# Moving tiles to one place of 512 bytes, and reordering the first loads and the last pair, in a hybrid GLA/HGRN2 encoder step

## The chip, the cores and the metric

The kernel runs on one core of a Trainium2 chip. The metric is the device time in microseconds of one execution; lower is better. Of the core's engines, TensorE (PE in the profile) multiplies matrices: one operand is loaded as weights (PEld), the other streams through in columns, and the result is added up in PSUM. VectorE (DVE), ScalarE (ACT) and GpSimd (POOL) do the elementwise work. Loads and stores between HBM and the on-chip memory SBUF are DMAs, issued from a queue of SyncE (SP) or of ScalarE. SBUF has 128 partitions; where a tile lies is one byte offset that holds in all partitions.

## The reference

One layer of an encoder with two parallel groups of heads runs over a prompt of 4096 frames and a sample of 64 frames, in float32. Cut to what matters:

```python
def mixer_layer(x, c, s_gla, s_hgrn, w_ada, b_ada, g_pre, w_in, w_alpha, b_alpha,
                g_on_gla, lb, g_on_hgrn, w_out, g_post):
    mod = jnp.einsum('bd,de->be', c, w_ada) + b_ada
    shift, scale, gate = jnp.split(mod, 3, axis=-1)
    h = rms_norm(x, g_pre) * (1 + scale[:, None]) + shift[:, None]
    p = jnp.einsum('btd,de->bte', h, w_in)          # 1024 -> 3600 columns
    q_a, k_a, v_a, z_a, a_lr, q_h, f_h, i_h, z_h = jnp.split(...)
    log_alpha = log_sigmoid(a_lr @ w_alpha + b_alpha) / GATE_TAU
    o_a, s_a = chunked_gla(q_a * GLA_DK ** -0.5, k_a, v_a, log_alpha, s_gla)
    f = lb + (1.0 - lb) * sigmoid(f_h)
    o_h, s_h = chunked_gla(silu(q_h), 1.0 - f, i_h, log(f), s_hgrn)
    o_a = rms_norm(o_a, g_on_gla) * silu(z_a)
    o_h = rms_norm(o_h, g_on_hgrn) * silu(z_h)
    o = jnp.einsum('bte,ed->btd', jnp.concatenate([o_a, o_h], axis=-1), w_out)
    return x + gate[:, None] * rms_norm(o, g_post), s_a, s_h
```

`chunked_gla` is a linear recurrence over frames, S = diag(exp g) S + k v, o = q S. The outputs are y for prompt and sample and the four final states.

## The kernel before

The prompt is cut into 16 groups of 256 frames, each of two tiles of 128; the sample's 64 frames go along with one group. There are four stages. The first group's projections run in `first_group`, written out by hand while the weights still arrive. Then 16 GLA groups, 16 HGRN2 groups, the gate z of the HGRN2 half for all tiles (`z_tile`), and the output projection (`project`), which works on pairs of frame tiles p = 0 to 15. A function `weave` mixes the projections of one group with the recurrence of the group before, so that TensorE always has matmuls at hand; within what is issued, a scheduler may still move instructions of different engines against each other.

Every product of h with a weight is made in three matmuls. `split` cuts a float32 operand into a rounded part and the rest (hi and lo, in float32r), and hi x hi, hi x lo and lo x hi are added up in PSUM. So every matmul loads 128 columns of weights anew. Two lines make most of the projections:

- L594 in `proj_feat`: loads 128 columns of the projection's weights (tiles `wa`, `wv`) and streams 256 frames of h (`hh`). GLA's q and k and HGRN2's f use `wa`, HGRN2's q uses `wv`.
- L606 in `tok_step`: loads 128 frames of h and streams the projection's weights, 512 columns (`wb`: v; `wa`: z of the last stage) or 264 (`wv`: z and the low-rank gate of GLA).

The output projection multiplies with seven products of 2x2 blocks instead of eight (a Strassen-Winograd scheme). `load_wout` makes the seven combinations of blocks of w_out (B11 to T4), each in four units of [128, 2 x 512], kept in freed `wv` and `wb` buffers and in twelve `wc`. `project` makes the combinations of the input (A11, A12, A22, S1 to S4) for each pair, in `wa` buffers (`s_tile`) and in two stage buffers `hs` (`a_tile`). L1391 in `product` is their matmul: it loads u, streams W. Each product fills one PSUM bank (`pj`, three deep, or `o`) in 12 matmuls. The last pair also holds the sample (`sample`, L614). `store` computes the norm over a row from the squares' sums, and adds x: sums (L1463), `rstd` (L82 to L93), L1472, and a DMA.

SBUF is handed out from two sides. From the left come `const`, `small`, the weights (`wa`, `wv`, `wb`, eight each), then the recurrence's tiles (later `wc` and the rest). From the right come the stage buffers, `e`, h (`hf`, `hh`) and x. A `wv` tile is 1056 words of 4 bytes, all other weights' tiles 1024; a stage buffer is 1056 words too. This puts the tiles, in bytes past a multiple of 512, at:

| tile | before |
|---|---|
| `hh`, `hf`, `xt`, `e` | 224 |
| `hs`, the two | 224, 352 |
| `wa`, `wb`, `wc`, recurrence (`A`, `K`, `v`, ...) | 320 |
| `wv`, eight buffers | 320, 448, 64, 192, twice over |
| `ident` (for transposes) | 128 |

hi and lo of one tile lie a multiple of 512 apart, but for the 264 columns, where the four pieces lie at 0, 32, 64 and 96 past the tile's place.

At the start, `setup` issues all loads on SP's queue: x, twelve small row vectors into `rows`, the identity, w_ada, and the first weights; small loads stand between the w_ada loads. `first_group` warms TensorE with matmuls on zeros (`warm`, L294), transposes the first 16 rows (L298), turns the first x tile (L313), then transposes all 52 rows (L319) into `col`, turns the second x tile, and goes on with the sums of w_ada (L241) and eight steps over k (L352, L606).

Of the kernel before, what the change touches and what calls it, by code (L numbers as in the profile page):

```python
# [6 lines left out]
F32 = mybir.dt.float32  # L7
F32R = mybir.dt.float32r
# [3 lines left out]
ALU = mybir.AluOpType  # L12
# [16 lines left out]
class Kernel:  # L29
# [41 lines left out]

    def rstd(self, ms, n, table=False):


        nc = self.nc
        r, w = ms.shape[0], ms.shape[1]
        yt = self.small.tile([P, 8], F32, name="nwt_y")
        ut = self.small.tile([P, 8], F32, name="nwt_u")
        mt = self.small.tile([P, 8], F32, name="nwt_m")
        y, u, m = yt[:r, :w], ut[:r, :w], mt[:r, :w]  # L80
        yi = yt.bitcast(I32)[:r, :w]
        nc.vector.tensor_scalar(m, ms, 1.0 / n, EPS, ALU.mult, ALU.add)  # L82
# [63 lines left out]
    def setup(self):  # L146
# [3 lines left out]
        self.wpool = self.pool(ctx, "w")  # L150

        self.wstage = self.pool(ctx, "wstage", 2, side="right")
        self.halves = []
# [14 lines left out]

        nc.scalar.preload_act_table_set("natural_log_exp_and_others")
        self.ident = c.tile([P, P], F32, name="ident")  # L170
# [16 lines left out]
        with ExitStack() as s:  # L187
            one = self.pool(s, "setup")
            ap = self.pool(s, "ada", 3)

            rows = one.tile([52, P], F32, name="rows")
            v = lambda a: a.rearrange("(k p) -> k p", p=P)
            self.x_load(0, [0])
            nc.sync.dma_start(rows[0:8], v(t["c_prompt"][0]))
            nc.sync.dma_start(rows[8:16], v(t["c_sample"][0]))
            nc.sync.dma_start(self.ident, t["ident"])
            self.x_load(0, [1])
            few = [
                (rows[16:32], v(t["b_ada"][0, : 2 * D])),
                (rows[32:40], v(t["g_pre"][0])),  # L200
                (rows[40:42], v(t["b_alpha"][0])),
                (rows[42:50], t["hgrn_lb_logits"].rearrange("r (k p) -> (r k) p", p=P)),
                (rows[50:51], t["g_onorm_gla"]),
                (rows[51:52], t["g_onorm_hgrn"]),
            ]
            ada = self.ada_load(ap, 0, few[:4])
            w = self.first_load(0)
            for dst, src in few[4:]:
                nc.sync.dma_start(dst, src)
            with self.tc.manual_schedule():  # L210
                self.first_group(ap, ada, w, rows)
            for _ in self.vs0:
                pass
# [3 lines left out]

    def ada_load(self, ap, k, few=()):

        sts = []  # L220
        for i in range(2):
            st = ap.tile([P, 4, 2, P], F32, name="ada_st", bufs=10)
            for e in range(2):
                src = self.t["w_ada"][0, i * 512 : i * 512 + 512, e * D + k * P : e * D + (k + 1) * P]
                self.nc.sync.dma_start(st[:, :, e, :], src.rearrange("(n p) c -> p n c", p=P))
                for dst, src in few[2 * i + e : 2 * i + e + 1]:
                    self.nc.sync.dma_start(dst, src)
            sts.append(st)
        return sts

    def first_group(self, ap, ada, w, rows):

# [59 lines left out]
        def warm(n):  # L292
# [4 lines left out]
        pr = self.ps("ms")  # L297
        nc.tensor.transpose(pr[:, :16], rows[:16], self.ident[:16, :16])  # L298
        warm(8)
        self.x_norm(0, [0])  # L300
        nc.vector.tensor_copy(col[:, :16], pr[:, :16])
        self.x_norm(0, [1])
        nc.vector.tensor_copy(
# [3 lines left out]
            self.fold4, self.ident.rearrange("p (n r) -> p r n", r=32)[:, 0:2], mybir.AxisListType.X, ALU.add  # L307
        )
        pts = [self.ps(n).rearrange("p (k t) -> p k t", k=2) for n in ("tp", "at", "at", "pj")]

# [6 lines left out]
        turn(0)  # L317
        pr = self.ps("ms")
        nc.tensor.transpose(pr[:, :52], rows, self.ident[:52, :52])  # L319
        turn(1)  # L320
# [3 lines left out]
        self.hf = [self.hp.tile([P, 2, T], F32, name="hf", bufs=4) for _ in range(4)]  # L324
        nc.vector.tensor_copy(col[:, 16:], pr[:, 16:52])
        nc.vector.tensor_scalar(col[:, 24:32], col[:, 24:32], 1.0, None, ALU.add)
        raw(0, nc.scalar)
        w_split(0, ws[0])
        am = ada_out(pa)
        ws.append(self.first_load(1))  # L330
# [11 lines left out]
        for k in range(KT):  # L342
# [31 lines left out]
            if k + 3 < KT:  # L374
                sts.append(self.ada_load(ap, k + 3))
            if k == KT - 3:
                self.x_load(1, [0, 1])
# [930 lines left out]
    def load_wout(self, room):  # L1308
# [62 lines left out]
    def project(self, ogs, rest):  # L1371

        nc, t, W = self.nc, self.t, self.W3
        ng = self.ng
        quarter = lambda u: u[:, :1024].rearrange("p (two k c) -> p two k c", two=2, k=4)
        s_tile = lambda: quarter(self.wunit("wa"))
        a_tile = lambda: quarter(self.stage_pair(F32R))

# [14 lines left out]
        with ExitStack() as s:  # L1393

            a21, a22 = [turn(o, n) for o, n in zip(ogs[2:], ("tp", "ms"))]
            a11, a12 = [turn(o, "at") for o in ogs[:2]]
            A11, A12 = a_tile(), a_tile()
            parts(A11, a11)
# [67 lines left out]
            def store(ss, ys, xs, dst, last=False):  # L1466

                r = ys[0].shape[0]
                add(ss[:r, 0:1], ss[:r, 0:1], ss[:r, 1:2])
                rs = self.rstd(ss[:r, 0:1], D, table=True)  # L1470
                for q in range(2):
                    nc.vector.scalar_tensor_tensor(xs[q], ys[q], rs, xs[q], ALU.mult, ALU.add)  # L1472
                    (nc.scalar if last and q else nc.sync).dma_start(dst[:, 512 * q : 512 * q + 512], xs[q])
# [26 lines left out]
            def sample(both, xs, gs):  # L1500
# [15 lines left out]
                store(ss, ys, xs, t["y_sample"][0, s0 : s0 + r])  # L1516

            ogs = og_load(1) if ng > 1 else None
            for p in range(ng):
# [8 lines left out]
                if more:  # L1528
# [4 lines left out]
                    add(w1, w21, a22)  # L1533

                b = self.ps("pj")
# [4 lines left out]
                if not more:  # L1540
                    sample(both, *rest_s)
                if more:
                    a11 = turn(ogs[0], "at")
                    A11 = a_tile()
                    w3, w2 = block(), block()
                    sub(w3, a11, w21)
                    sub(w2, w1, a11)
                    parts(A11, a11)
                    parts(S3, w3, nc.gpsimd)
                    parts(S1, w1, nc.gpsimd)  # L1550
                    parts(S2, w2)

                b = self.ps("pj")
                product(b, cur["S2"], "T2")
                u2 = add(tmp(), b, p1)
                if more:
                    A22, A12 = s_tile(), a_tile()
                    parts(A22, a22)
                    a12 = turn(ogs[1], "at")
                    parts(A12, a12)  # L1560
                    ogs = og_load(p + 2) if p + 2 < ng else None

                b = self.ps("pj")
                product(b, cur["S3"], "T3")
                u3 = add(tmp(), b, u2)
                if more:
                    S4 = s_tile()
                    w4 = sub(block(), a12, w2)
                    parts(S4, w4, nc.gpsimd)
                if p == ng - 2:  # L1570
# [19 lines left out]
                scale(y21, y21, 0)  # L1590
                store(ss[1], [y21, y22], xs[2:], rows(p, 1), not more)
                if p == ng - 2:
                    both = turn_sample(ogs)
                if more:
                    cur = dict(A11=A11, A12=A12, A22=A22, S1=S1, S2=S2, S3=S3, S4=S4)

# [207 lines left out]
```

## Time and profile before

| | us |
|---|---|
| time, median of 3 runs | 2065.14 (2062.38 to 2065.37) |
| time of the profiled execution | 2065.15 |
| its span | 2063.4 |
| granted TensorE clock, share of full speed | 0.995 |
| PE busy | 2033.4 (99%) |
| DVE busy | 1513.0 (73%) |
| ACT busy | 1088.9 (53%) |
| first matmul of the eight steps (L352) | at 19.0 |
| last matmul's end, by the chain | at 2054.4 |

The span runs from the first to the last instruction's record; the time has a little around it. Lines like L594 are those of the kernel before. A row such as `L594 PE MATMUL ps_pj<-hh,wa 128*128 128x256 f32 x2784 | 360.8, 284` reads: line, engine, operation, what it writes from what, the tile of weights, the shape streamed, how often; busy us in total, mean ns of one.  A row of the timeline has start, length, engine, line, operation, count, and in brackets how long the engine had been idle and what ended that. A row of the chain has start, length, and who led.

### The profile page before, as it was taken

To read this page: it belongs to the slowest core of one execution; us is meant where nothing else is said; L and a number is where in the kernel's file an instruction comes from. 1 tells how busy PE (TensorE), PEld (TensorE's weight loads), DVE (VectorE), ACT (ScalarE), POOL (GpSimd) and SP (SyncE) were. 2 spreads that over 40 slices of the span, in tenths; PEclk is the share of its full clock that TensorE was granted. 3 is DMA by queue.
4 is the path that set the end of the run, shared out by engine and by line. 5 is a ranking of instruction groups with operands and counts; after the bars stand their busy time and mean duration, and the time that the engine had idled before them with its cause. 6 is when DMAs were issued, how large, how long until landed. Compare 5 with 4: busy or idle time off the path is not lost.

```text
span 2063.4 us, 47068 instructions
## 1 busy us (share of the span) xinstructions
PE 2033.4 (99%) x17404; PEld 1796.0 (87%) x17404; DVE 1513.0 (73%) x4740; ACT 1088.9 (53%) x3207; POOL 304.1 (15%) x782
## 2 busy tenths in 40 slices
PE   8999999999999999999999999999999999999998
PEld 6888899999999888989999999999978888888886
DVE  4776777767777678777777877877786667767675
ACT  4676666777667565444444444444545544434332
POOL 0111111111111121111111111111110002333321
PEclk9999999999999999999999999999999999999999
DMA  9332222232222231011111111100246654534443
GB/s 296 97 77 64 62 58 57 64 73 62 58 56 75 82 118 44 32 37 60 52 37 51 46 65 32 38 32 32 63 139 212 216 194 149 170 131 167 140 143 103
DMA packets 236086, 190.10 MB, mean 92 GB/s; under 512 B 138208, under 2 KB 160196, under 8 KB 235856
## 3 DMA queue, kind: packets, MB, share of 16 engines
q1 hardware_dynamic: 235712, 186.83, 29.9%
q8 instruction: 137, 2.24, 0.5%
q14 instruction: 93, 0.76, 0.1%
q10 hardware_dynamic: 144, 0.26, 0.0%
HBM read 126.59 MB, written 60.43 MB: 91 GB/s over the span
## 4 chain that ended last, share of the span: by engine, by line
PE 91%; DVE 4%; ACT 3%; DMA 1%; issue 1%; POOL 0%; SPq 0%; DVEq 0%; ACTq 0%; POOLq 0%
PE ps_pj L606 32%; PE ps_pj L594 25%; PE ps_pj L1391 13%; PE ps_at L674 3%; PE ps_at L1003 2%; PE ps_ms L805 2%; PE ps_o L789 2%; PE ps_o L781 2%; PE ps_o L1391 2%; PE ps_at L910 1%; PE ps_tp L754 1%; PE ps_pj L614 1%; PE ps_at L1382 1%; PE ps_ms L781 1%; PE ps_pj L352 1%
## 5 line engine op out<-in xcount | busy, mean ns | idle before, releaser
L594 PE MATMUL ps_pj<-hh,wa 128*128 128x256 f32 (+1 forms) x2976 | 390.8, 286 | 0.6 <-ACT hh L102 0.4
L606 PE MATMUL ps_pj<-wb,hh 128*128 128x512 f32 x1536 | 386.0, 402 | 0.5 <-POOL wb L103 0.5
L594 PEld LDWEIGHTS ps_pj<-hh,wa 128*128 128x128 f32 x2976 | 369.1, 189 | 5.3 <-issue 1.7
L606 PEld LDWEIGHTS ps_pj<-wb,hh 128*128 128x128 f32 x1536 | 281.7, 189 | 66.1 <-issue 2.9
L594 PE MATMUL ps_pj<-hh,wv 128*128 128x256 f32 (+1 forms) x1536 | 196.2, 285 | 0.0
L594 PEld LDWEIGHTS ps_pj<-hh,wv 128*128 128x128 f32 x1536 | 187.4, 189 | 10.0 <-issue 9.7
L606 PE MATMUL ps_pj<-wv,hh 128*128 128x264 f32 x1464 | 191.1, 287 | 0.0
L606 PEld LDWEIGHTS ps_pj<-wv,hh 128*128 128x128 f32 x1464 | 181.5, 188 | 3.6 <-ACT e L1099 2.4
L606 PE MATMUL ps_pj<-wa,hh 128*128 128x512 f32 x768 | 182.3, 396 | 0.0
L606 PEld LDWEIGHTS ps_pj<-wa,hh 128*128 128x128 f32 x768 | 143.3, 188 | 35.0 <-issue 0.8
L1249 ACT ACTIVATE g<-ps_pj 128x256 f32<-128x256 f32 (+1 forms) x128 | 49.6, 388 | 219.3 <-PE ps_pj L594 214.3
L103 DVE TENSOR_TENSOR hh<-hf,hh 128x512 fp32r<-128x512 f32 (+1 forms) x188 | 129.9, 696 | 16.3 <-ACT hh L102 13.6
L102 ACT CAST hh<-hf 128x512 fp32r<-128x512 f32 (+1 forms) x188 | 117.2, 624 | 41.6 <-PE ps_pj L606 22.8
L816 DVE SCALAR_TENSOR_TENSOR S<-S,T,ps_ms 128x128 f32<-128x128 f32 x186 | 56.1, 340 | 81.4 <-PE ps_ms L805 81.4
L953 DVE TENSOR_TENSOR wst<-wst,T 128x160 f32<-128x160 f32 (+4 forms) x480 | 107.9, 265 | 1.4
L977 ACT ACTIVATE A<-Ac,member 128x128 f32<-128x128 f32 x256 | 80.0, 389 | 47.2 <-DVE Ac L971 47.2
L1451 ACT ACTIVATE sq<-e 128x512 bf16<-128x512 f32 x64 | 40.4, 631 | 121.0 <-DVE e L1463 121.0
L1391 PE MATMUL ps_pj<-wc,wa 128*128 128x512 f32 x384 | 98.9, 392 | 0.0
L1454 POOL TENSOR_TENSOR e<-e,gg 128x512 f32<-128x512 f32 x32 | 41.6, 1299 | 367.8 <-ACT sq L1451 367.8
L984 POOL COPY T<-T 128x16 f32<-128x16 f32 (+1 forms) x32 | 7.8, 244 | 543.7 <-DVE Qg L845 401.6
L1391 PEld LDWEIGHTS ps_pj<-wc,wa 128*128 128x128 f32 x384 | 72.0, 188 | 16.3
L971 DVE COPY_PREDICATED Ac<-mask,ps_at 128x112 f32<-128x112 uint8 (+6 forms) x448 | 82.5, 223 | 2.1 <-PE ps_at L1003 1.0
(349 smaller groups left out, 4028.2 us busy)
## 6 DMA issues: line engine op xcount, KB each, us to landing
hf<-h_d SPq DMA_DIRECT2D x128, 256.0 KB
h_d<-hf SPq DMA_DIRECT2D x64, 256.0 KB
oh_d<-e SPq DMA_DIRECT2D x64, 256.0 KB
xq<-in_x_prompt_dram SPq DMA_DIRECT2D x64, 256.0 KB
out_y_prompt_dram<-xq SPq DMA_DIRECT2D x63, 256.0 KB
xt<-in_x_prompt_dram SPq DMA_DIRECT2D x448, 32.0 KB
wst<-in_w_in_dram SPq DMA_DIRECT2D x36, 256.0 KB
e<-oh_d SPq DMA_DIRECT2D x33, 256.0 KB
```

The lines of the kernel that those rows point to most:

```text
L102: self.nc.scalar.copy(hi, src)
L103: (eng or self.nc.vector).tensor_tensor(lo, src, hi.bitcast(F32), ALU.subtract)
L594: self.nc.tensor.matmul(ps[:, :T], a, b, start=i == 0, stop=i == n - 1)
L606: self.nc.tensor.matmul(ps[:r, : c1 - c0], a, b, start=kt == 0 and i == 0, stop=kt == KT - 1 and i == 2)
L674: nc.tensor.transpose(pt[:, i * P : (i + 1) * P], D[:, c + i, :], self.ident)
L781: mm = nc.tensor.matmul(po[h], A[:, c * 4 + h, :], v, start=h < n, stop=St is None and h == 4 - n)
L816: nc.vector.scalar_tensor_tensor(Sn[:, g, :], St[:, g, :], T[:, c * G + g, 0:1], pd[:, g, :], ALU.mult, ALU.add)
L953: nc.vector.tensor_tensor(parts(dst), parts(src), t.unsqueeze(3).to_broadcast(shape), ALU.mult)
L971: nc.vector.copy_predicated(Ach[:, :, 4 * a :].rearrange("p h (j m) -> p h j m", m=4), self.mask[:CL, : 8 - a].unsqueeze(1).unsqueeze(3).t ...
L977: nc.scalar.activation(Ah[:, :, 32 * b : 32 * b + 32], Ach, AF.Copy, scale=self.member[:CL, 8 + b : 9 + b])
L1249: nc.scalar.activation(sg, pf[:, :T], AF.Sigmoid)
L1391: nc.tensor.matmul(bank, u[:, a, kt, :], W[name][kt][:, b], start=kt + i == 0, stop=kt + i == 5)
```

## The change

It has three parts.

*Places.* A tile `pad` of 32 bytes is put ahead of all others on the right side, so all tiles there move by -32. In `quad_norm`, `q_ss` and `q_half` have two buffers instead of four, four tiles of 32 bytes less in `small`, so all that lies behind on the left moves by -128. h, `wa`, `wb` and `wc` then lie at 192 past a multiple of 512, `wv` at 192, 320, 448, 64. In `load_wout` those parts of w_out that are kept in four of the eight `wv` buffers start 32 words (128 bytes) further in, and the second of `a_tile`'s two buffers too: by the order in which the buffers are taken, the units in `wv` lie at 192 or 448, and the two `hs` at 192 and 448.

*First loads.* c_prompt, c_sample, b_ada and g_pre go on ScalarE's queue, ahead of its table load. Their 40 rows stay in `rows` and are transposed once, ahead of the first x tile; the other 12 rows go to a tile `later`, loaded after the first weights and transposed in the second of the eight steps. Five warming matmuls stand between the two x tiles where the transpose stood. The copy of the sums (`ada_out`) is issued ahead of `w_split(0)`, and the second x tile's norm behind the work on `col`.

*Last pair.* A function `last` orders the products of pair 15 as A11 B11, S2 T2, (sample), S1 T1, S4 B22, A12 B21, S3 T3, A22 T4, instead of A11 B11, A12 B21, (sample), S2 T2, S3 T3, S1 T1, S4 B22, A22 T4. The first half of the rows is stored after A12 B21. For the last store, one half's sum of squares is scaled ahead, so that one VectorE operation adds the other (`rest` in `rstd`).

```diff
-    def rstd(self, ms, n, table=False):
+    def rstd(self, ms, n, table=False, rest=None):
...
-        nc.vector.tensor_scalar(m, ms, 1.0 / n, EPS, ALU.mult, ALU.add)
+        if rest is None:
+            nc.vector.tensor_scalar(m, ms, 1.0 / n, EPS, ALU.mult, ALU.add)
+        else:
+            nc.vector.scalar_tensor_tensor(m, ms, 1.0 / n, rest, ALU.mult, ALU.add)
...
+        self.pool(ctx, "pad", side="right").tile([P, 8], F32, name="pad")
         self.wstage = self.pool(ctx, "wstage", 2, side="right")
...
-        nc.scalar.preload_act_table_set("natural_log_exp_and_others")
...
-            rows = one.tile([52, P], F32, name="rows")
+            rows, later = one.tile([40, P], F32, name="rows"), one.tile([12, P], F32, name="later")
             self.x_load(0, [0])
-            nc.sync.dma_start(rows[0:8], v(t["c_prompt"][0]))
-            nc.sync.dma_start(rows[8:16], v(t["c_sample"][0]))
             nc.sync.dma_start(self.ident, t["ident"])
             self.x_load(0, [1])
-            few = [
+            for dst, src in [
+                (rows[0:8], v(t["c_prompt"][0])),
+                (rows[8:16], v(t["c_sample"][0])),
                 (rows[16:32], v(t["b_ada"][0, : 2 * D])),
                 (rows[32:40], v(t["g_pre"][0])),
...
-            ada = self.ada_load(ap, 0, few[:4])
+            ]:
+                nc.scalar.dma_start(dst, src)
+            nc.scalar.preload_act_table_set("natural_log_exp_and_others")
+            ada = self.ada_load(ap, 0)
             w = self.first_load(0)
-            for dst, src in few[4:]:
+            for dst, src in [
+                (later[0:2], v(t["b_alpha"][0])),
+                (later[2:10], t["hgrn_lb_logits"].rearrange("r (k p) -> (r k) p", p=P)),
+                (later[10:11], t["g_onorm_gla"]),
+                (later[11:12], t["g_onorm_hgrn"]),
+            ]:
                 nc.sync.dma_start(dst, src)
...
-        nc.tensor.transpose(pr[:, :16], rows[:16], self.ident[:16, :16])
+        nc.tensor.transpose(pr[:, :40], rows, self.ident[:40, :40])
         warm(8)
         self.x_norm(0, [0])
-        nc.vector.tensor_copy(col[:, :16], pr[:, :16])
-        self.x_norm(0, [1])
+        nc.vector.tensor_copy(col[:, :40], pr[:, :40])
...
+        nc.vector.tensor_scalar(col[:, 24:32], col[:, 24:32], 1.0, None, ALU.add)
+        self.x_norm(0, [1])
...
         turn(0)
-        pr = self.ps("ms")
-        nc.tensor.transpose(pr[:, :52], rows, self.ident[:52, :52])
+        warm(5)
         turn(1)
...
         raw(0, nc.scalar)
+        am = ada_out(pa)
         w_split(0, ws[0])
-        am = ada_out(pa)
...
+            if k == 1:
+                pr = self.ps("ms")
+                nc.tensor.transpose(pr[:, :12], later, self.ident[:12, :12])
+                nc.vector.tensor_copy(col[:, 40:], pr[:, :12])
...
-        ss, half, rs = [self.small.tile([P, 8], F32, name=n) for n in ("q_ss", "q_half", "q_rs")]
+        ss, half, rs = [
+            self.small.tile([P, 8], F32, name=n, bufs=b) for n, b in (("q_ss", 2), ("q_half", 2), ("q_rs", 4))
+        ]
...
-            u = self.wunit(rooms.pop(0)[0]) if rooms else room.tile([P, 1024], F32R, name="wc", bufs=12)
-            return u[:, :1024].rearrange("p (two c) -> p two c", two=2)
+            tag, i = rooms.pop(0) if rooms else ("wc", 0)
+            u = room.tile([P, 1024], F32R, name="wc", bufs=12) if tag == "wc" else self.wunit(tag)
+            o = 32 if tag == "wv" and i in (2, 4, 5, 7) else 0
+            return u[:, o : o + 1024].rearrange("p (two c) -> p two c", two=2)
...
-        a_tile = lambda: quarter(self.stage_pair(F32R))
+        a_tile = lambda second: quarter(self.stage_pair(F32R), 32 if second else 0)
...
+            def last(p, cur, p1, xs, ss):
+                u2, b5 = tmp(), self.ps("o")
+                def out(q, n, u, j, a, to=None):
+                    b = self.ps("pj")
+                    product(b, cur[n], u)
+                    y = add(self.etile(), b, a)
+                    square(ss[j], q, y)
+                    to = y if to is None else to
+                    scale(to, y, q)
+                    return to
+                b = self.ps("pj")
+                product(b, cur["S2"], "T2")
+                add(u2, b, p1)
+                sample(both, *rest_s)
+                product(b5, cur["S1"], "T1")
+                u4 = add(tmp(), b5, u2)
+                y12 = out(1, "S4", "B22", 0, u4)
+                y11 = out(0, "A12", "B21", 0, p1)
+                store(ss[0], [y11, y12], xs[:2], rows(p, 0))
+                b = self.ps("pj")
+                product(b, cur["S3"], "T3")
+                u3 = add(tmp(), b, u2)
+                y22 = add(self.etile(), b5, u3)
+                square(ss[1], 1, y22)
+                scale(y22, y22, 1)
+                y21 = out(0, "A22", "T4", 1, u3, tmp())
+                store(ss[1], [y21, y22], xs[2:], rows(p, 1), True)
```

More of the change, by code (lines that the diff above doesn't have):

```diff
@@ L189, in setup @@
             ap = self.pool(s, "ada", 3)
-            rows = one.tile([52, P], F32, name="rows")
+            rows, later = one.tile([40, P], F32, name="rows"), one.tile([12, P], F32, name="later")
             v = lambda a: a.rearrange("(k p) -> k p", p=P)
             self.x_load(0, [0])
-            nc.sync.dma_start(rows[0:8], v(t["c_prompt"][0]))
-            nc.sync.dma_start(rows[8:16], v(t["c_sample"][0]))
             nc.sync.dma_start(self.ident, t["ident"])
             self.x_load(0, [1])
-            few = [
+            for dst, src in [
+                (rows[0:8], v(t["c_prompt"][0])),
+                (rows[8:16], v(t["c_sample"][0])),
                 (rows[16:32], v(t["b_ada"][0, : 2 * D])),
                 (rows[32:40], v(t["g_pre"][0])),
[L201 to L205, printed above, removed]
-            ada = self.ada_load(ap, 0, few[:4])
-            w = self.first_load(0)
-            for dst, src in few[4:]:
+            ]:
+                nc.scalar.dma_start(dst, src)
+            nc.scalar.preload_act_table_set("natural_log_exp_and_others")
+            ada = self.ada_load(ap, 0)
+            w = self.first_load(0)
+            for dst, src in [
[4 more added lines that the diff above has]
+            ]:
                 nc.sync.dma_start(dst, src)
             with self.tc.manual_schedule():
-                self.first_group(ap, ada, w, rows)
+                self.first_group(ap, ada, w, rows, later)
             for _ in self.vs0:
@@ L216, in first_load, with ada_load @@
         return self.load_w(k, [(C_QA, 512)], self.etile), self.load_w(k, [(C_ZA, 528)])
-    def ada_load(self, ap, k, few=()):
+    def ada_load(self, ap, k):
         sts = []
@@ L225, in ada_load, with first_group @@
                 self.nc.sync.dma_start(st[:, :, e, :], src.rearrange("(n p) c -> p n c", p=P))
-                for dst, src in few[2 * i + e : 2 * i + e + 1]:
-                    self.nc.sync.dma_start(dst, src)
             sts.append(st)
         return sts
-    def first_group(self, ap, ada, w, rows):
+    def first_group(self, ap, ada, w, rows, later):
         nc, col = self.nc, self.col
@@ L324, in first_group @@
         self.hf = [self.hp.tile([P, 2, T], F32, name="hf", bufs=4) for _ in range(4)]
-        nc.vector.tensor_copy(col[:, 16:], pr[:, 16:52])
-        nc.vector.tensor_scalar(col[:, 24:32], col[:, 24:32], 1.0, None, ALU.add)
         raw(0, nc.scalar)
+        am = ada_out(pa)
         w_split(0, ws[0])
-        am = ada_out(pa)
         ws.append(self.first_load(1))
@@ L1374, in project @@
         ng = self.ng
-        quarter = lambda u: u[:, :1024].rearrange("p (two k c) -> p two k c", two=2, k=4)
+        quarter = lambda u, o=0: u[:, o : o + 1024].rearrange("p (two k c) -> p two k c", two=2, k=4)
         s_tile = lambda: quarter(self.wunit("wa"))
-        a_tile = lambda: quarter(self.stage_pair(F32R))
+        a_tile = lambda second: quarter(self.stage_pair(F32R), 32 if second else 0)
         def turn(src, tag, r=P):
@@ L1396, in project @@
             a11, a12 = [turn(o, "at") for o in ogs[:2]]
-            A11, A12 = a_tile(), a_tile()
+            A11, A12 = a_tile(False), a_tile(True)
             parts(A11, a11)
@@ L1468, in store @@
                 r = ys[0].shape[0]
-                add(ss[:r, 0:1], ss[:r, 0:1], ss[:r, 1:2])
-                rs = self.rstd(ss[:r, 0:1], D, table=True)
+                rest = None
+                if last:
+                    rest = ss[:r, 1:2]
+                    nc.vector.tensor_scalar(rest, rest, 1.0 / D, EPS, ALU.mult, ALU.add)
+                else:
+                    add(ss[:r, 0:1], ss[:r, 0:1], ss[:r, 1:2])
+                rs = self.rstd(ss[:r, 0:1], D, table=True, rest=rest)
                 for q in range(2):
@@ L1533, in project @@
                     add(w1, w21, a22)
+                if not more:
+                    last(p, cur, p1, xs, ss)
+                    break
                 b = self.ps("pj")
@@ L1539, in project @@
                 scale(y11, y11, 0, eng=nc.gpsimd)
[L1540 to L1551, printed above, removed]
+                a11 = turn(ogs[0], "at")
+                A11 = a_tile(False)
+                w3, w2 = block(), block()
+                sub(w3, a11, w21)
+                sub(w2, w1, a11)
+                parts(A11, a11)
+                parts(S3, w3, nc.gpsimd)
+                parts(S1, w1, nc.gpsimd)
+                parts(S2, w2)
                 b = self.ps("pj")
@@ L1555, in project @@
                 u2 = add(tmp(), b, p1)
[L1556 to L1561, printed above, removed]
+                A22, A12 = s_tile(), a_tile(True)
+                parts(A22, a22)
+                a12 = turn(ogs[1], "at")
+                parts(A12, a12)
+                ogs = og_load(p + 2) if p + 2 < ng else None
                 b = self.ps("pj")
@@ L1565, in project @@
                 u3 = add(tmp(), b, u2)
[L1566 to L1569, printed above, removed]
+                S4 = s_tile()
+                w4 = sub(block(), a12, w2)
+                parts(S4, w4, nc.gpsimd)
                 if p == ng - 2:
@@ L1590, in project @@
                 scale(y21, y21, 0)
-                store(ss[1], [y21, y22], xs[2:], rows(p, 1), not more)
+                store(ss[1], [y21, y22], xs[2:], rows(p, 1))
                 if p == ng - 2:
                     both = turn_sample(ogs)
-                if more:
-                    cur = dict(A11=A11, A12=A12, A22=A22, S1=S1, S2=S2, S3=S3, S4=S4)
+                cur = dict(A11=A11, A12=A12, A22=A22, S1=S1, S2=S2, S3=S3, S4=S4)
     def og_half(self, p, j, q, ap=None):
```

## The prediction

> **What bounds the kernel now.** First the page: span, busy time of each engine, and who leads the chain of work that ended last.
>
> ```profile
> span 2063.4 us, 47068 instructions
> PE 2033.4 (99%) x17404; PEld 1796.0 (87%) x17404; DVE 1513.0 (73%) x4740; ACT 1088.9 (53%) x3207; POOL 304.1 (15%) x782
> PE 91%; DVE 4%; ACT 3%; DMA 1%; issue 1%; POOL 0%; SPq 0%; DVEq 0%; ACTq 0%; POOLq 0%
> ```
>
> TensorE is busy nearly throughout, and 91% of the chain is its own work. Busy time of matmuls is modelled, so the second view is the waits of TensorE (line, releaser, us in total, times, longest; the first and the last of 18 rows).
>
> ```profile
> PE ps_o L781 <- ACT A L922: 3.3, 4, 2.4
> ...
> PE ps_pj L594 <- DVE hh L103: 0.2, 1, 0.2
> ```
>
> The 18 rows add up to 21 us, 1% of the span. A nanosecond saved per matmul therefore comes out of the span, except in the 9% of the chain where others lead. Third, the groups by shape: how many matmuls of each kind there are.
>
> ```profile
> L606 PE MATMUL ps_pj<-wb,hh 128*128 128x512 f32 x1536 | 386.0, 402 | 0.5 <-POOL wb L103 0.5
> L594 PE MATMUL ps_pj<-hh,wa 128*128 128x256 f32 x2784 | 360.8, 284 | 0.6 <-ACT hh L102 0.4 <-DVE hh L103 0.2
> L606 PE MATMUL ps_pj<-wv,hh 128*128 128x264 f32 x1464 | 191.1, 287 | 0.0
> L606 PE MATMUL ps_pj<-wa,hh 128*128 128x512 f32 x768 | 182.3, 396 | 0.0
> L594 PE MATMUL ps_pj<-hh,wv 128*128 128x256 f32 x1440 | 181.5, 283 | 0.0
> ```
>
> The mean there is one matmul's length with its drain, not its pace. The pace comes from pairs of timeline rows that start at the same matmul and end some matmuls later, all inside one accumulation.
>
> ```profile
> 980.17 0.63 PE L606 MATMUL ps_pj<-wb,hh 128*128 128x512 f32 x2
> 980.17 4.83 PE L606 MATMUL ps_pj<-wb,hh 128*128 128x512 f32 x20
> 956.78 0.52 PE L594 MATMUL ps_pj<-hh,wa 128*128 128x256 f32 x3
> 956.78 2.53 PE L594 MATMUL ps_pj<-hh,wa 128*128 128x256 f32 x20
> 1018.46 0.51 PE L594 MATMUL ps_pj<-hh,wv 128*128 128x256 f32 x3
> 1018.46 3.31 PE L594 MATMUL ps_pj<-hh,wv 128*128 128x256 f32 x27
> ```
>
> With 512 moving columns: (4.83 - 0.63) / 18 = 233.3 ns. With 256: (2.53 - 0.52) / 17 = 118.2 ns when the weights come from wa, (3.31 - 0.51) / 24 = 116.7 ns when they come from wv. Same shape, same h, two paces: what differs is that wa lies at 320 past a multiple of 512 and wv at four places in turn. The chain shows the like with 512 columns, in the output projection (each row is start to start, so it holds everything the matmuls cost).
>
> ```profile
> 1986.39 2.79 PE ps_pj L1391 x12
> 1992.85 2.79 PE ps_pj L1391 x12
> 1995.65 2.72 PE ps_o L1391 x12
> 2040.66 5.52 PE ps_pj L1391 x24
> 2046.18 2.72 PE ps_o L1391 x12
> 2048.90 5.49 PE ps_pj L1391 x24
> ```
>
> The product into ps_o takes 2.72 / 12 = 226.7 ns a matmul; there both operands lie at 320, or 256 apart. The first row's hs parts lie at 352 against 320, the second's first parts (wv) at 448 against 320: 232.5 ns. In L606 h lies at 224 against 320: 233.3 ns. So the trace holds three unequal pairs that are slow and an equal one that is fast, and no L594 group and no 512-wide L606 group has the equal one. By the mechanism that these rows suggest, the weights that are loaded for the next matmul and the columns that stream in for this one get in each other's way unless they are at one place (or 256 apart).
>
> The Trainium skill, "TensorE: Matmul & The Clock Gate", Part 2, speaks against this: TensorE has two independent read ports, and loading the next weights doesn't steal read bandwidth from the running matmul. By that rule the places are worth nothing, and what is left of the change is the start and the end, 2062.1 us, the third rival below. The rows above (226.7 against 233.3 ns in one shape) do not agree with it, but they don't prove the cause either.
>
> **The change part by part.** Two of the four-deep tiles in the pool small become two-deep: 4 x 32 bytes less, so all that lies behind moves by -128. The pad moves the right side by -32. Then h is at 192, wa, wb and wc at 192, wv at 192, 320, 448, 64; the output's parts in wv and hs get 128 more where they need it, and stand at 192 or 448. These are the terms:
>
> *512 columns, L606, 1536 + 768 = 2304 matmuls, from 233.3.* After, between 226.7 and the (5.52 + 2.72 + 5.49) / 60 = 228.8 ns of the last five products, which holds their starts and a few wv parts 128 off. I take 228.0: 5.3 ns x 2304 = 12.2 us (bounds 4.5 and 6.6 ns: 10.4 and 15.2).
>
> *256 columns with wa, L594, 2784 matmuls, from 118.2.* No row shows this shape at one place. The best end is half of the 512-wide, 113.3 ns; the other end is no gain, 118.2 (a loss is a rival). wv's 116.7 at mixed places lies between. I take the middle, 115.5, since the wv row is about midway too: 2.7 x 2784 = 7.5 us (0 to 13.6).
>
> *256 columns with wv, 1440.* Half of them come to stand at one place or 256 apart, half at 128 from it. Bounds: 720 at 113.3 gain 2.4 us; 720 at 118.2 lose 1.1 us. I take 0, the row's own mean.
>
> *264 columns, 1464.* wv's offsets run through all multiples of 32 against h before and after: 0.
>
> *Output projection.* Three products of each pair go from 2.79 to 2.72 us: 0.07 x 3 x 16 = 3.4 us (2 to 4.5).
>
> *Transposes.* The identity stays at 128 while the A, K and og that it turns move to 192. Before, xt at 224 and og at 320 cost the same, so I take 0:
>
> ```profile
> 73.42 0.44 PE ps_tp L528 x4
> 1992.41 0.44 PE ps_at L1382 x4
> ```
>
> Sum on TensorE 12.2 + 7.5 + 3.4 = 23.1; with the 91% of the chain, 21.0 us. The rest is absorbed where VectorE or ScalarE lead.
>
> *The start.* These rows are of the timeline (start, us, engine):
>
> ```profile
> 0.73 1.28 ACT L169 ACT_TABLE_LOAD   x1 [0.73 <-PEq L1791]
> 1.18 0.36 SPq L194 DMA_DIRECT2D rows<-in_c_prompt_dram  x1
> 4.17 1.06 ACT L476 ACTIVATE hf<-xt 128x1024 bf16<-128x1024 f32 x1 [2.15 <-DMA xt<-in_x_prompt_dram]
> 6.20 2.12 PE L294 MATMUL ps_pj<-zero 128*128 128x512 f32 x8
> 8.05 1.06 ACT L476 ACTIVATE hf<-xt 128x1024 bf16<-128x1024 f32 x1 [2.07 <-DMA xt<-in_x_prompt_dram]
> 10.47 0.75 DVE L481 TENSOR_SCALAR xt<-xt,nwt_y 128x1024 f32<-128x1024 f32 x1
> 12.50 0.32 PE L319 MATMUL ps_ms<-ident,rows 52*128 52x52 f32 x1 [3.31 <-DMA rows<-in_g_onorm_hgrn_dram]
> 13.85 0.61 ACT L102 CAST wa<-e 128x512 fp32r<-128x512 f32 x1
> 14.65 1.93 PE L241 MATMUL ps_o<-ada_st,cs 128*32 128x256 f32 x16
> 21.04 1.47 PE L241 MATMUL ps_o<-ada_st,cs 128*32 128x256 f32 x16
> ```
>
> Before, TensorE stands 3.31 us until the last row vector has landed, and then works slowly. After, that transpose waits for nothing late. Ahead of the second x tile SP issues two small loads less (0.36 us the first; some 0.7 both, with their gaps), and two less between the w_ada loads. The tile's norm ends at 11.2 us now (10.47 + 0.75) and at 10.5 then, about when five warming matmuls (2.12 / 8 x 5 = 1.3 us) are done. The second turn begins at 10.5 to 11.3 instead of 12.8 (12.50 + 0.32): about 1.5 us. The sums behind it may take 1.47 instead of 1.93. I take 2.0 us; bounds 0.5 (if w_ada lands late and takes the wait over) and 3.0.
>
> What the start adds: four issues on ScalarE ahead of its table load, four times about 0.4 as on SP. They end with the load at 0.73 + 1.6 + 1.28 = 3.6, covered by ScalarE's wait for x until 4.17; without that cover they would put the first norm off by up to 1.6 us. The four loads left on SP behind first_load put off the w_ada issues behind them as the old ones did. The first cast (0.61) now stands behind the copy of the sums on ScalarE; TensorE's turn of the sums covers it, and if not, up to 0.6 us of the gain goes. `later` costs one more small transpose (as L319, 0.32 us) and a copy. The two-deep q_ss and q_half are written again only a group later, when their readers are long done: 0.
>
> *The end.* After the last matmul:
>
> ```profile
> 2054.42 0.69 DVE e L1463
> 2057.00 0.69 DVE L1454 TENSOR_TENSOR e<-e,gg 128x512 f32<-128x512 f32 x1
> 2059.03 1.41 DVE L1472 SCALAR_TENSOR_TENSOR xq<-e,nwt_y,xq 128x512 f32<-128x512 f32 x2
> 2060.47 0.38 ACTq L1473 DMA_DIRECT2D out_y_prompt_dram<-xq  x1
> ```
>
> From 2054.40 to the last issue are 6.1 us. 1.9 of them lie between the end of the first add (2055.11) and the scaling (2057.00), behind the store of the other half of the rows. With that store 5.5 us earlier and one small add less, the tail could shrink to 4.3 us. But VectorE, which takes over all scaling of this pair from POOL, still has y22's add and scale (0.69 each) and the earlier store (1.41) to do within the last product's 2.7 us. I take 1.0 us (0 to 1.8). The order of the products moves the sample part by no more than one product.
>
> **The sum.** 21.0 + 2.0 + 1.0 = 24.0 us off the profiled execution's 2065.15 us (its span of 2063.4 and 1.75 around it, which stay), equal to the median of the runs, 2065.14: 2041.15, say 2041 us.
>
> **Rivals.** *More:* everything that comes to one place runs at 226.7 or half of it. 15.2 + 13.6 + 2.4 + 3.4 = 34.6, x 0.91 = 31.5, + 3.0 = 34.5: 2031 us. For it: those products hold 226.7 over whole runs. Against: no L594 row comes near 113.3.
>
> *Less:* only 512 columns gain, at their lower bound: (10.4 + 3.4) x 0.91 + 3.0 = 15.6: 2050 us. For it: the 256-wide paces differ by only 1.5 ns today.
>
> *It doesn't do what it says:* the paces come from something else than the place, such as which stage it is (the 2.72 is the product into ps_o, which has a bank of its own). Then start and end remain: 2062.1 us.
>
> *Slower:* at one place the weight load and a short stream collide each time, since a 256-wide matmul leaves the load no slack. Place: L594, 2784 + 720 = 3504 matmuls, 3.19 us for each ns on the chain. The other terms gain (12.2 + 3.4) x 0.91 + 3.0 = 17.2, so it decides from 5.4 ns (123.6 instead of 118.2); at 8 ns the time is 2065.15 - 17.2 + 25.5 = 2073 us. Against: the 264-wide group meets every place in turn, the equal one too, and stays at 2.91 / 24 = 121.3 ns, that is 117.6 for 256 columns:
>
> ```profile
> 128.98 2.91 PE ps_pj L606 x24
> ```
>
> **Numbers.** A change of 0.2% (4.1 us) is about what a measurement of this kernel tells from none. Forecast (2034 to 2047) 0.45, more 0.2, less 0.2, nothing from the places 0.09, slower 0.06. Faster: 0.85, same 0.09, slower 0.06. The range runs from the rival with more, less the 3 us of the bounds at start and end, to 2056, where the 256-wide gain nothing, wv loses its 1.1 and only 80% of the rest reaches the span.
>
> **What would show it.** Right: L606 near 228 ns by the same pair of rows, L594 with wa below 117, ps_pj products at 2.72, all other shapes as before; the wait of L319 gone, the sums of L241 beginning at 12 to 13 us instead of 14.65; last issue less than 5.5 us after the last matmul. Wrong: L606 still at 233; or paces down, but new waits of TensorE on VectorE in the groups; or L594 above 120.

## The result, and the profile after

| | before | after |
|---|---|---|
| time, median us (runs) | 2063.85 (6, 2062.20 to 2065.52) | 2053.54 (6, 2050.82 to 2054.28) |
| span of the profiled execution | 2063.4 | 2052.5 |

The ratio is 0.9947, 95% interval 0.9934 to 0.9960: faster by 10.3 us where 24 were forecast. The time lies at the slow end of the forecast's range, but less than half of the gain came. Line numbers have moved: L594 is now L603, L606 L615, L1391 L1404, L241 L246, L352 L355; in the kernels of the experiments they move by a few lines more.

The page of after, in the same three lines as before:

```profile
span 2052.5 us, 47070 instructions
PE 2025.4 (99%) x17409; PEld 1802.1 (88%) x17409; DVE 1514.7 (74%) x4742; ACT 1088.5 (53%) x3207; POOL 301.6 (15%) x780
PE 88%; DVE 4%; ACT 4%; DMA 2%; SPq 1%; issue 1%; POOL 0%; DVEq 0%; ACTq 0%; POOLq 0%
```

TensorE is still the bound. The groups by shape, with busy us in total and mean ns after the bar:

```profile
L615 PE MATMUL ps_pj<-wb,hh 128*128 128x512 f32 x1536 | 377.9, 397 | 0.5 <-POOL wb L106 0.5
L603 PE MATMUL ps_pj<-hh,wa 128*128 128x256 f32 x2784 | 365.1, 286 | 0.6 <-ACT hh L105 0.4 <-DVE hh L106 0.2
...
L603 PE MATMUL ps_pj<-hh,wv 128*128 128x256 f32 x1440 | 184.1, 285 | 0.0
L615 PE MATMUL ps_pj<-wa,hh 128*128 128x512 f32 x768 | 177.9, 391 | 0.0
```

Against the rows of before: the two 512-wide groups fell from 386.0 to 377.9 and from 182.3 to 177.9, 12.5 us together. The two 256-wide ones rose from 360.8 to 365.1 and from 181.5 to 184.1, 6.9 us together. So the change won on the long products and lost on the short ones.

The mean there (397 ns) is longer than the pace, since the records of successive matmuls overlap. The pace is read from the chain, where a row runs from the start of its first matmul to the start of what follows. Two rows of the chain of before:

```profile
162.35 4.27 PE ps_pj L594 x36
...
1560.58 140.00 PE ps_pj L606 x600
```

and of after:

```profile
163.43 4.31 PE ps_pj L603 x36
...
1558.57 136.04 PE ps_pj L615 x600
...
2033.52 8.17 PE ps_pj L1404 x36
```

512 columns: 140.00 / 600 = 233.3 ns before, 136.04 / 600 = 226.7 after. 256 columns with wa: 4.27 / 36 = 118.6 before, 4.31 / 36 = 119.7 after. The output's products into ps_pj: 8.17 / 36 = 226.9, where the slow ones were at 2.79 / 12 = 232.5. These two rows, x600 of the stage of `z_tile` (512 columns; called the last stage below, the last in which h is read) and x36 of one early GLA group (256 columns with wa), are compared in every kernel below. The row of 36 is a small sample: by the whole group of 2784 the loss is 4.3 us, 1.5 ns a matmul, where the two rows of 36 differ by 1.1.

Of TensorE's waits, the long one for the last row vector (L319, 3.3 us) is gone; smaller ones have grown or come up (line, releaser, total, times, longest). All 18 rows add up to 18.8 us, against 21 before.

```profile
PE ps_ms L303 <- DMA rows<-in_g_pre_dram: 1.7, 1, 1.7
...
PE ps_ms L258 <- ACT e L252: 1.2, 3, 0.5
...
PE ps_pj L355 <- ACT hh L273: 0.8, 1, 0.8
```

### The profile page after: what moved, and what is told of

It reads as the page before. It is cut to its first block, busy times and chain, and to the rows that moved or that the text cites. A ratio compares the mean times of both kernels' runs of the same rounds, so it can differ in the third digit from the quotient of the medians.

```text
span 2052.5 us, 47070 instructions
## 1 busy us (share of the span) xinstructions
PE 2025.4 (99%) x17409; PEld 1802.1 (88%) x17409; DVE 1514.7 (74%) x4742; ACT 1088.5 (53%) x3207; POOL 301.6 (15%) x780
## 4 chain that ended last, share of the span: by engine, by line
PE 88%; DVE 4%; ACT 4%; DMA 2%; SPq 1%; issue 1%; POOL 0%; DVEq 0%; ACTq 0%; POOLq 0%
PE ps_pj L615 31%; PE ps_pj L603 25%; PE ps_pj L1404 13%; PE ps_at L683 3%; PE ps_at L1012 2%; PE ps_ms L814 2%; PE ps_o L798 2%; PE ps_o L1404 2%; PE ps_o L790 2%; DMA wst<-in_w_in_dram 1%; PE ps_at L919 1%; PE ps_tp L763 1%; PE ps_pj L623 1%; PE ps_at L1395 1%; PE ps_ms L790 1%
## 5 line engine op out<-in xcount | busy, mean ns | idle before, releaser
L603 PE MATMUL ps_pj<-hh,wa 128*128 128x256 f32 (+1 forms) x2976 | 395.0, 288 | 0.6 <-ACT hh L105 0.4
L615 PE MATMUL ps_pj<-wb,hh 128*128 128x512 f32 x1536 | 377.9, 397 | 0.5 <-POOL wb L106 0.5
L603 PEld LDWEIGHTS ps_pj<-hh,wa 128*128 128x128 f32 x2976 | 373.4, 191 | 5.1 <-issue 1.7
L615 PEld LDWEIGHTS ps_pj<-wb,hh 128*128 128x128 f32 x1536 | 280.6, 188 | 59.7 <-issue 2.9
L603 PE MATMUL ps_pj<-hh,wv 128*128 128x256 f32 (+1 forms) x1536 | 198.8, 287 | 0.0
L603 PEld LDWEIGHTS ps_pj<-hh,wv 128*128 128x128 f32 x1536 | 189.8, 190 | 9.8 <-issue 9.6
L615 PE MATMUL ps_pj<-wv,hh 128*128 128x264 f32 x1464 | 190.9, 287 | 0.0
L615 PEld LDWEIGHTS ps_pj<-wv,hh 128*128 128x128 f32 x1464 | 181.3, 188 | 3.6 <-ACT e L1108 2.4
L615 PE MATMUL ps_pj<-wa,hh 128*128 128x512 f32 x768 | 177.9, 391 | 0.0
L615 PEld LDWEIGHTS ps_pj<-wa,hh 128*128 128x128 f32 x768 | 143.3, 188 | 30.7 <-issue 0.8
L1404 PE MATMUL ps_pj<-wc,wa 128*128 128x512 f32 x384 | 98.1, 390 | 0.0
L1404 PEld LDWEIGHTS ps_pj<-wc,wa 128*128 128x128 f32 x384 | 72.0, 188 | 15.2
```

What stands on the lines that cost most here:

```text
L603: self.nc.tensor.matmul(ps[:, :T], a, b, start=i == 0, stop=i == n - 1)
L615: self.nc.tensor.matmul(ps[:r, : c1 - c0], a, b, start=kt == 0 and i == 0, stop=kt == KT - 1 and i == 2)
L1404: nc.tensor.matmul(bank, u[:, a, kt, :], W[name][kt][:, b], start=kt + i == 0, stop=kt + i == 5)
```

## The experiments

Two theories at first. A: the pace hangs on the distance between the place of the loaded weights and that of the streamed columns, and the equal place is good for long streams and bad for short ones. B: the place of h by itself sets it. "Distance" below is L603's: the place of the tile `wa` minus that of h, modulo 256. In L615 h is the one that is loaded, so there the sign is the other way round.

**h moved back (e1_h224) and on (e2_h160), distances -32 and +32.** All else is the changed kernel.

```diff
-        self.pool(ctx, "pad", side="right").tile([P, 8], F32, name="pad")     # e1: no pad, h at 224
+        self.pool(ctx, "pad", side="right").tile([P, 16], F32, name="pad")    # e2: h at 160
```

> The changed kernel without the 32-byte pad: h, hs and x at 224, all weights stay at 192 (weights of L603 lie 32 bytes below h). Theory A, the distance from the stream to the next weights (modulo 256) sets the pace: wv at 32 below h ran at 114.7 ns before, so all of L603 with wa comes to 115 ns (changed kernel 119.7, before 118.5), with wv back to 116.7; L615 with 512 columns now streams 32 below its weights and goes to 230 to 232 ns (changed 226.7, before 233.3). Sum against the changed kernel: -13 -3.5 +10 to +13 and +2 in the output projection, so 2049 to 2053 us. Theory B, the place of h itself sets the pace of L603 (224 good, 192 bad): 118.5 ns with wa, as before the change, and L615 stays at 226.7 since its stream still lies at 192: 2047 to 2049 us.

> The changed kernel with a pad of 64 bytes instead of 32: h, hs and x at 160, weights at 192 (32 above h). Theory A: a distance of +32 for L603 (no row has it) and of -32 for L615. If nearness alone counts, L603 gains as with -32 (115 ns); if the sign counts, L603 is slower than the 119.7 of distance 0 and L615 with 512 columns is at 229 to 230 (the 256-wide row at -32 doubled). Theory B: L603 somewhere other than 118.5, L615 at 226.7.

e1: 2058.36 us, ratio 0.9975 (0.9966 to 0.9985). e2: 2062.99, ratio 0.9999 (0.9990 to 1.0009). The chain of e1:

```profile
161.65 4.21 PE ps_pj L602 x36
...
1557.56 140.00 PE ps_pj L614 x600
```

and of e2:

```profile
160.42 4.26 PE ps_pj L603 x36
...
1561.45 140.00 PE ps_pj L615 x600
```

Both expectations for the time of e1 were too low by 5 us or more, and both had L615 faster than it ran. e1 and e2 lose the whole 512-wide gain: 32 bytes apart is as slow (233.3) as 96 apart was. The streamed tile of L615 stands at 192 in both as in the changed kernel, so the streamed tile's place alone isn't it. Nor is B what happens: it had L615 at 226.7 ns in both and L603 at 118.5 in e1. The 256 columns go to 4.21 / 36 = 116.9 ns at -32 and to 118.3 at +32: both better than the 119.7 at distance 0, and -32 better than before. The rows of the weight loads move with that: line, shapes, count, busy us and mean ns; before, after and e1 in turn.

```profile
L594 PEld LDWEIGHTS ps_pj<-hh,wa 128*128 128x128 f32 x2976 | 369.1, 189 | 5.3 <-issue 1.7 <-ACT hh L102 0.6 <-DVE hh L103 0.4
```

```profile
L603 PEld LDWEIGHTS ps_pj<-hh,wa 128*128 128x128 f32 x2976 | 373.4, 191 | 5.1 <-issue 1.7 <-ACT hh L105 0.6 <-DVE hh L106 0.4
```

```profile
L602 PEld LDWEIGHTS ps_pj<-hh,wa 128*128 128x128 f32 x2976 | 365.5, 188 | 5.5 <-issue 1.7 <-ACT hh L105 0.6 <-DVE hh L106 0.4
```

The load of 128 columns while 256 stream (320 in 192 of the 2976) takes 189, 191 and 188 ns, in the order of the paces. With 512 columns of `wb` the load's mean hardly moves (189 ns before, 188 after), though the pace moves by 6.6 ns.

**The parts apart: start and end alone (e3_start_end), places alone (e4_places).** e3 is the changed kernel with its pad, its two-deep tiles and its shifts of 32 words undone; e4 is the kernel before with these alone.

```diff
 # e3, against after
-        self.pool(ctx, "pad", side="right").tile([P, 8], F32, name="pad")
...
-            self.small.tile([P, 8], F32, name=n, bufs=b) for n, b in (("q_ss", 2), ("q_half", 2), ("q_rs", 4))
+        ss, half, rs = [self.small.tile([P, 8], F32, name=n) for n in ("q_ss", "q_half", "q_rs")]
...
```

> The changed kernel with the three parts of the places undone (no pad, four-deep q_ss and q_half, no offset in the output's parts): only the first loads and the last pair differ from the kernel before. If the terms add up: 2.9 us faster than before (start 2.0, end 0.9), about 2061 us, with L603 and L615 at the paces of before. A rival, that the start's or the end's gain was in truth the places': nothing, 2064 us.

> The kernel before with the places alone (pad, two-deep q_ss and q_half, offsets in the output's parts). If the terms add up: 12.3 + 3.8 us gained in 512 columns, 8 us lost in 256 columns, so 8 us faster than before, about 2056 us, L606 at 226.7 and L594 with wa at 119.7 ns.

e3: 2061.95, ratio 0.9992 (0.9983 to 1.0002): 1.6 us, not told from nothing by the interval. e4: 2055.87, ratio 0.9964 (0.9952 to 0.9977): 7.6 us. The first is less than the 2.9 expected, the second as expected (8). Together they make 9.2, near the 10.3 of the whole. The chain of e4 has the paces of after, without its start and end:

```profile
162.93 4.31 PE ps_pj L597 x36
...
1557.95 136.01 PE ps_pj L609 x600
```

**More distances (e6_h000, e7_h064), and distance 0 at another place (e8_all224).**

```diff
-        self.pool(ctx, "pad", side="right").tile([P, 8], F32, name="pad")
+        self.pool(ctx, "pad", side="right").tile([P, 56], F32, name="pad")   # e6: h at 0, distance -64
+        self.pool(ctx, "pad", side="right").tile([P, 40], F32, name="pad")   # e7: h at 64, distance 128
# e8: no pad, and
-  ("q_half", 2)
+  ("q_half", 3)
```

> Weights of the changed kernel at 192 of 512, h pushed to 0 by a pad of 224 bytes: distance from h to weights 192, which is -64 of 256. Distance theory: 512 columns at 233.3 ns as at every unequal place so far; 256 columns with wa between the 116.6 ns of -32 and the 118.5 ns of 96. Rival (h's own place sets the pace, 0 being the start of a row): 512 columns at 226.7 ns.

> As the run with h at 0, with h at 64 by a pad of 160 bytes: distance 128 of 256. Distance theory: 512 columns at 233.3 ns; 256 columns with wa near the 118.5 ns of 96. If the distance counts by another period (128 instead of 256), 512 columns take 226.7 ns and 256 columns 119.7 ns, as at an equal place.

> No pad; a third buffer of q halves pushes the weights to 224 instead of pushing h to 192: all at 224. Distance theory: the pace of the changed kernel, 226.7 ns for 512 columns and 119.7 ns for 256 with wa, and its time, 2053. Rival (the place 192 itself): 512 columns at 233.3 ns.

One run each, beside one of before at 2062.55: e6 2058.14, e7 2063.20, e8 2054.88. The chains of e6, e7 and e8:

```profile
160.62 4.24 PE ps_pj L603 x36
...
1555.99 140.00 PE ps_pj L615 x600
```

```profile
162.05 4.27 PE ps_pj L603 x36
...
1561.77 139.43 PE ps_pj L615 x600
```

```profile
163.11 4.31 PE ps_pj L602 x36
...
1558.94 136.04 PE ps_pj L614 x600
```

Everything at 224 has the two paces of everything at 192, to the last digit, so the place 192 itself isn't it, and h at 0 helps nothing for 512 columns. In one table: ns a matmul from those rows, and below them busy us of whole groups. Half of wv's tiles stand at the distance named, half 128 further on.

| distance | -64 (e6) | -32 (e1) | 0 (after, e8) | +32 (e2) | +96 (before) | 128 (e7) |
|---|---|---|---|---|---|---|
| 512 columns | 233.3 | 233.3 | 226.7 | 233.3 | 233.3 | 232.4 |
| 256 columns, wa | 117.8 | 116.9 | 119.7 | 118.3 | 118.6 | 118.6 |
| all 2784 with wa, us | 359.2 | 357.0 | 365.1 (e8 365.3) | 360.6 | 360.8 | 362.8 |
| all 1440 with wv, us | 178.2 | 180.5 | 184.1 (e8 182.6) | 183.8 | 181.5 | 182.9 |

The equal place is the best of six for 512 columns and the worst of six for 256 with wa, by the rows and by the whole groups.

Distance and width aren't all, though. The quickest 256 columns of all runs are those with wv in e6, whose tiles stand at -64 and +64:

```profile
L603 PE MATMUL ps_pj<-hh,wv 128*128 128x256 f32 x1440 | 178.2, 281 | 0.0
```

From start to start over the three matmuls of one step of k (one tile of wv), the median there is 113.3 ns a matmul, at -64 as at +64, where wa at -64 takes 117.8. That is the best end that the prediction had for this shape, at a place that it didn't consider. What sets wa and wv apart at one distance isn't shown.

**Width or role (e5_split).** In L615 the weights stream and h is loaded, in L603 the other way round. To tell width from role, the 512-column products are cut into halves:

```diff
+            n = c1 - c0
+            parts = [(0, n)] if n < 512 or (kt == 0 and i == 0) else [(0, 256), (256, 512)]
+            for p0, p1 in parts:
-            self.nc.tensor.matmul(ps[:r, : c1 - c0], a, b, ...)
+                self.nc.tensor.matmul(ps[:r, p0:p1], a, b[:, p0:p1], ...)
```

> The changed kernel; in the token step each 512-column product, but for the first of each accumulation, is issued as two products of 256 columns, at the same places. Role theory (at an equal place a product that streams h is quick and one that streams a weight tile is slow): two halves take about 2 x 113.3 = 226.7 ns, as the whole one did, and the time rises by little more than the issue of some 2300 more products. Width theory (equal place is quick for 512 columns and slow for 256, whoever streams): two halves take about 2 x 119.7 = 239.4 ns, and the 2304 products lose some 12.7 ns each, 29 us.

2080.97 us in one run, against 2062.55 of before: 27 us above the changed kernel's 2053.54. Its chain in the last stage, 25 whole products and 1150 halves:

```profile
1574.99 143.83 PE ps_pj L618 x1175
```

(143.83 - 25 x 0.2267) / 1150 = 120.1 ns a half, next to the 119.7 of L603 at the same distance. So at the equal place it doesn't matter who streams: two halves cost 240 ns where the whole cost 226.7. Halves at another distance weren't run.

**A place for each width (e9_mix; e10_mixz; e12_mixz beside e11_after).** If distance and width are all there is, both gains can be had: h and `wb` at 224, `wa` and `wv` at 192, and in the last stage, where only 512 columns read h, h moved within its slot to equal `wa` modulo 256.

```diff
 # e9: no pad; ahead of wb, and ahead of wc (wc at 448)
+        self.wpool.tile([P, 8], F32, name="wpad", bufs=1)
+        room.tile([P, 56], F32, name="wcpad", bufs=1)
 # e10 = e12: besides, in split_h for the last stage, groups of 256
+                u = self.hp.tile([P, 5 * GROUP], F32R, name="hh", bufs=5)[:, 56 : 56 + 4 * GROUP]
```

> The changed kernel with two places: h and wb at 224, wa and wv 32 bytes below, at 192 (the distance of the run with h at 224). Distance theory, against the changed kernel: the 256 columns win 7.9 + 2.3 us with wa and wv and 1 us in the first group, wb's 512 columns stay at 226.7 ns, wa's 512 columns go back to 233.3 (+4.5 us), the output's products of wb with wa and of the token parts with wv and wc lose about 3 us: 2053.5 - 11.2 + 7.5 = some 2050 us. If a place for each width brings nothing (the 256 columns slow down by something else in the change), 2053.5 + 7.5 = 2061.

> As the run with two places, and in the last stage, where only 512-column products read h, h stands 224 bytes further into its slot, at 448, which is 192 of 256, as wa (but for the one group of 320 columns). Distance theory: wa's 512 columns back at 226.7 ns but for an eighth, some 4 us less than the run with two places: about 2046 us. If the slot's place counts and not that of the data in it, as the run with two places.

> The changed kernel once more, beside the two-place kernel with h moved in the last stage, on one chip: 2053.5 us, 0.995 of the kernel before.

> The two-place kernel with h moved in the last stage, once more. By the sums of TensorE's groups it should be 2 us below the changed kernel (the 256 columns win 10 us, the output's unequal places lose 4, the rest differs by run), 2051.5; if the difference of the earlier runs was that between chips, both at 2053.

e9: 2054.52, ratio 0.9952 (0.9937 to 0.9967). e10: 2051.50, ratio 0.9937 (0.9920 to 0.9953). On one chip: the changed kernel 2053.26 (2052.65 to 2054.76, ratio 0.9950, 0.9936 to 0.9963) and e12, the kernel of e10, 2051.09 (2050.51 to 2051.55, ratio 0.9937, 0.9924 to 0.9949). The five runs of one all lie below the five of the other, so e12 is the fastest, if by only 2.2 us. Its chain:

```profile
161.14 4.20 PE ps_pj L607 x36
...
1550.22 136.01 PE ps_pj L619 x600
```

```profile
1739.52 2.78 PE ps_pj L1409 x12
...
1748.74 2.77 PE ps_o L1409 x12
1751.51 8.32 PE ps_pj L1409 x36
```

116.7 and 226.7 ns: one kernel has the best pace for 512 columns and wa's best for 256, as expected. The price stands in the second fence: no output product is at 2.72 any more; 8.32 / 36 = 231.1 ns. That includes those whose parts are in `wc`, at 448 against 192: equal modulo 256, and yet 231, while `wv` at 448 against the same 192 runs at 226.7 in the same kernel. e9's expectation had 3 us for this; summed over L1409, each matmul from its start to the next one's, it is 4.6 (314.7 against 310.1 in the changed kernel). That is 1.6 of the 4.5 and 5.5 us by which the expected 2050 and 2046 were too low; the rest isn't settled. The step from e9 to e10, forecast at 4 us, was 3.0.

## Why the prediction was wrong, step by step

- **512 columns, 12.2 us: right.** 12.5 by the groups. The steady pace is 226.7, the range's best end (228.0 was taken), and the starts of the products, which do not get faster, make the mean what was forecast.
- **256 columns with wa, 7.5 us of gain: the step that failed.** It took the 512-wide rule over to a shape for which, as it said itself, no row showed the equal place, with "half of the 512-wide, 113.3" as the best end and "no gain" as the other. Measured: +4.3 us, 1.5 ns a matmul. With wv, 0 forecast, +2.6 (+1.1 in e8 and e4), at or past the bound of 1.1 of loss. In the forecast's sum the 7.5 counted as 7.5 x 0.91 = 6.8; together with the loss of 6.9 that makes 13.7 us, as much as lies between 24.0 and 10.3. The other terms' misses are smaller and nearly cancel. The slower rival had the sign, but asked for 5.4 ns, and its reason, a short stream with no slack beside the weight load, isn't shown by any run. Against that rival stood the 264 columns, which "meets every place in turn" and stays at 121.3: a mean over places, which could not show what one place costs. Sorted by the places of each matmul's own operands, those at the equal place take 120.4 ns in before, about 1 ns less than the group: as far as places that change with nearly every matmul can show it, the equal place isn't slow for 264 columns.
- **The mixed row misread.** wv's 116.7 at mixed places against wa's 118.2 was taken as a point on the way to the 113.3 of an equal place, though none of wv's four places equals that of h. Half of wv stood at -32 (192 and 448 against h at 224), half at +96 as wa; sorted so, by steps of k, the medians are 114.7 and 118.7 ns. The change moved that half to 0 and the other from +96 to 128, so the group got slower.
- **Output, 3.4 us: right.** 313.9 to 310.1, 3.8 by L1391 and L1404 summed from start to start.
- **Times 0.91: not seen.** The terms by the groups (-12.5 + 6.9 - 3.8), the end (-0.9) and the start (0.3 in this execution, see below) make 10.6 us of the span's 10.9. Nothing has to have been absorbed; the discount took 2.1 us from a sum that was too high for another reason. That the time still fell into the range is in part luck: its end of 2056 stood on no gain for the 256 columns with wa, a loss of 1.1 us with wv and 80% of the rest, not on a loss of 6.9.
- **The start, 2.0 us: there at first, and not kept.** The timeline of after, at the start:

```profile
11.21 1.40 PE L299 MATMUL ps_pj<-zero 128*128 128x512 f32 x5
...
13.41 1.07 PE L246 MATMUL ps_o<-ada_st,cs 128*32 128x256 f32 x16
...
16.99 1.56 PE L355 MATMUL ps_pj<-hh,wa 128*128 128x256 f32 x8 [0.83 <-ACT hh L273]
```

The sums begin at 13.41 instead of 14.65 (12 to 13 was forecast, so a little late) and L355 at 16.99 instead of 19.03, 2.0 us earlier. But the wait of 0.83 on ScalarE is new, and 50 us later less is left. The turn of x nearest to 68 us, in the timelines of before, of after, and of after's second profile (e11_after):

```profile
68.40 0.60 PE L528 MATMUL ps_tp<-ident,xt 128*128 128x128 f32 x4
```

```profile
68.07 0.60 PE L537 MATMUL ps_tp<-ident,xt 128*128 128x128 f32 x4
```

```profile
66.64 0.60 PE L537 MATMUL ps_tp<-ident,xt 128*128 128x128 f32 x4
```

0.33 us in one execution, 1.76 in the other: it differs by run, and e4, which has the start of before, is 0.9 ahead of it at this turn (67.48). e3's 1.6 (start and end together, 3.0 forecast) fits that. What sets it in these 50 us wasn't tried.

- **The end, 1.0 us: right.** The timeline of after, all engines:

```profile
2042.88 1.52 PE L1404 MATMUL ps_pj<-wc,wa 128*128 128x512 f32 x6
...
2043.43 1.41 DVE L1491 SCALAR_TENSOR_TENSOR xq<-e,nwt_y,xq 128x512 f32<-128x512 f32 x2
...
2044.77 0.69 DVE L1467 TENSOR_TENSOR e<-e,gg 128x512 f32<-128x512 f32 x1
2045.37 0.69 DVE L1476 TENSOR_TENSOR e<-ps_pj,tmp 128x512 f32<-128x512 f32 x1
...
2049.59 0.38 ACTq L1492 DMA_DIRECT2D out_y_prompt_dram<-xq  x1
```

The last matmul ends at 2042.88 + 1.52 = 2044.40; the last issue is 5.2 us later (6.1 before, under 5.5 forecast). The add that waits for that matmul starts only at 2045.37, behind the earlier store's scaling and y22's multiplication on VectorE, as the prediction named it.

On the Trainium skill's rule in "TensorE: Matmul & The Clock Gate", Part 2, that a weight load doesn't steal read bandwidth from the running matmul: what the prediction drew from it, that the places are worth nothing, doesn't hold in these runs. e8 and e1 differ in places and one spare buffer alone, and one shape takes 226.7 against 233.3 ns, another 119.7 against 116.9. The third rival, that the paces come from something else than the place, falls with e4, where the places alone take 7.6 us off. Whether loads and streams get in each other's way at all, and which, isn't shown: the load's mean moves (188 to 191 ns), but that may be the effect as well as the cause.

## What to carry to other kernels

A pace that is measured for one shape holds for that shape: before a rule on operands' places is taken over to another width, one run at that place and width tells its sign, and here it was the opposite one. Where most of a kernel is back-to-back matmuls that each load new weights, places are worth a sweep of a few offsets per shape, as 3% of a matmul is at stake; and shapes that want different distances need different tiles moved, not one common place. Such a sweep is worth more than a rule: why the quickest place found for 256 columns, wv's in e6, is quick isn't explained here. A row that is a mean over mixed places, as of wv or of the 264 columns, is no evidence on any one of them.

## What the runs showed of the hardware

- A matmul with 512 columns of float32r and new weights takes 226.7 ns with both operands at one place modulo 256 bytes, and 232.4 to 233.3 at the five other distances that were run; 32 bytes are enough to lose it. Modulo 256 isn't all of it: `wc` at 448 against `wa` at 192 ran at 231.3 in e12 (three matmuls from start to start in 694 ns, the median), `wv` at 448 against it at 226.7.
- With 256 columns and `wa` it is 116.7 to 119.7 ns, slowest at the equal place; halves of 512 columns there behave as 256 (120.1). With `wv`, whose place changes from step to step, 113.3 at -64 and +64 (e6).
